# Forgetting attention on one Trainium2 core: score and value items issued in pairs

## The chip, the cores and the metric

The kernel runs on one core of one Trainium2 chip. The metric is the device time of one execution in microseconds, from launch to end, of that core. The kernel before takes 2528.2 us in the median of three runs (2527.69 to 2528.59).

## What is computed

One layer of a streaming encoder over 2048 tokens of width 1024, in 32-bit floats: RMS norm and a combined projection; forgetting attention in 8 heads of width 64 beside a pooling branch; cross attention to 256 memory tokens; a gated feed-forward block. The change touches the forgetting attention alone:

```python
c = jnp.cumsum(jax.nn.log_sigmoid(f_logit), axis=-1)
for start in range(0, S, Q_BLOCK):
    end = start + Q_BLOCK
    s = jnp.einsum('bhqd,bhkd->bhqk', q[:, :, start:end], k[:, :, :end]) * scale
    s = s + c[:, :, start:end, None] - c[:, :, None, :end]
    s = jnp.where(kpos[None, :] <= qpos[:, None], s, -jnp.inf)
    p = jax.nn.softmax(s, axis=-1)
    outs.append(jnp.einsum('bhqk,bhkd->bhqd', p, v[:, :, :end]))
```

## The kernel before

Matrix products in full precision are made of products of a high and a low part (`hi` is a rounded copy, `lo` the difference). Each engine has its own instruction queue and works it off in order. The stages follow one another: projection, pooling and its share of the output projection, forgetting attention, output projection with cross attention, feed-forward. The changed stage runs from about 523 to 903 us of the span.

**Units and items.** The attention is cut into 32 units (h, b): head h (0 to 7) and block b (0 to 3) of 512 query rows. Two generators give out the work in items:

- A *score item* (`score_items`, line 769) is one tile of 128 queries by up to 512 keys: two products of TensorE (PE, line 791) into the PSUM tile `sps` (three buffers), and one operation of VectorE (DVE, line 793) that adds the forget bias, writes the scores to the SBUF row tile `s{b}g{g}` and keeps the row's minimum. GpSimd (POOL) makes the masked bias `cm` (line 782) for a diagonal tile. When a row of tiles is complete, a small reduction on DVE (line 798) and one or two exponentials on ScalarE (ACT, line 803, at most 1024 columns each) follow by appointment.
- A *value item* (in `value_items`, line 843) is one chunk of 128 keys by 512 queries: up to four 128x128 transposes on PE (the helper `turned`, line 55) into the PSUM tile `tp` (three buffers); the rounded copy `ph` on ACT and the difference `pl` on DVE (the helper `sub_hi`, line 63; five buffers each); and, LAG = 3 items later, two products with the values V into `acc` (`weighted`, line 854). Every eighth chunk (`SHARE`) inside a unit is split by POOL in place of DVE (lines 887 to 889) and has a lag of 5.

A unit has 4(b+1) items of each kind, so there are 320 score items and 320 value items. On the diagonal the last four chunks of a unit have 4, 3, 2 and 1 transposes. At a unit's end `drain` issues the products still waiting, and `finish` adds the two halves of `acc` on ACT and DVE.

**The order.** PE, DVE and ACT keep the order in which the Python code issues (`in_order`). A loop draws a score item while `lead` is under LEAD = 22, else a value item, and calls `tick()` after each; `later(n, fn)` issues `fn` n ticks on (EX = 7 for an exponential, 2 more for the row's second one). After 22 scores the loop gives one score item and one value item in turn. In `value_items`, `wait` holds the chunks whose products are still to come; `step()` is called once for each chunk and issues what has come of age:

```python
wait.append([lag, (j, qa, ph, pl)])
step()
yield True
```

POOL and SyncE (SP, which starts most DMAs) take no part in the fixed order.

Of the kernel before, what the change touches and what calls it, by code (L numbers as in the profile page):

```python
# [40 lines left out]
def block_kernel(ctx: ExitStack, tc: tile.TileContext, x, xT, memT, cols, rows, w_qkvf, w_p, w_pool, w_out,  # L41
# [9 lines left out]
    def f(ap):  # L51
        return ap.bitcast(F32)

    def turned(out, src):
        return pe.transpose(out.bitcast(F32R), src, identr[:])  # L55

    def needs(inst, *others):

        for o in others:
            tc.add_manual_dep(inst.ins, o.ins.name, mybir.DependencyInfo(mybir.DependencyClass.Sync, mybir.DependencyReason.DATA))  # L60

    def sub_hi(lo, src, hi, eng=None):
        (eng or dve).tensor_tensor(out=lo, in0=src, in1=f(hi), op=ALU.subtract)  # L63
# [655 lines left out]
    LEAD, LAG = 22, 3  # L719
# [23 lines left out]
    with ExitStack() as c0:  # L743
# [7 lines left out]
        def later(n, fn):  # L751
            due.append([n, fn])

        def tick():
            for e_ in due:
                e_[0] -= 1
            for e_ in [e_ for e_ in due if e_[0] <= 0]:
                due.remove(e_)
                e_[1]()

        def row_tile(b, g, dt):

            n, w_ = f"s{b}g{g}", min(1024, 512 * (b + 1) - 1024 * g)
            t_ = spool.tile([P, 4 * w_ + 2], dt, tag=n, name=n, bufs=1)
            if dt == F32R:
                dve.memset(f(t_[:, 4 * w_:]), 0.0)
            return t_[:, :4 * w_].rearrange("p (q c) -> p q c", q=4)
# [59 lines left out]
        def finish(unit, acc):  # L827
            h, b = unit["u"]
            fo = tpool.tile([DH, 512], F32, tag="fo", name="fo", bufs=3)
            act.copy(fo[:], acc[DH:, :])  # L830
            dve.tensor_tensor(out=fo[:], in0=acc[:DH, :], in1=fo[:], op=ALU.add)
            later(SCALE, lambda: scale(unit, fo))
# [10 lines left out]
        def value_items(unit):  # L843
            h, b = unit["u"]
            v = unit["head"][4]
            nk = 4 * (b + 1)
            acc = aps.tile([P, 512], F32, tag="acc", name="acc", bufs=2)
            wait = []
            state = dict(n=0)

            def weighted(j, qa, ph, pl):
                for pm in (ph, pl):
                    state["n"] += 1
                    pe.matmul(acc[:, qa * P:], lhsT=v[:, j, :], rhs=pm[:, qa * P:], start=state["n"] == 1,  # L854
                              stop=state["n"] == 2 * nk)

            def step(flush=False):
                for e_ in list(wait):
                    e_[0] -= 1
                    if e_[0] < 0 or flush:  # L860
                        wait.remove(e_)
                        weighted(*e_[1])

            for j in range(nk):
                if j % 8 == 0:
                    exps = unit["exps"][j // 8]
                    assert len(exps) == 4
                    rows = row_tile(b, j // 8, F32R)
                q0 = max(0, j - 4 * b)
                qa = min(q0, 2)  # L870
                tp = tps.tile([P, 512], F32, tag="tp", name="tp", bufs=3)
                for q in range(q0, 4):
                    t_ = turned(tp[:, q * P:(q + 1) * P], rows[:, q, j % 8 * P:(j % 8 + 1) * P])
                    if j % 8 == 0:
                        needs(t_, exps[q])
                ph = tpool.tile([P, 512], F32R, tag="ph", name="ph", bufs=5)
                pl = tpool.tile([P, 512], F32R, tag="pl", name="pl", bufs=5)
                if qa < q0:
                    for t_ in (ph, pl):
                        pool.memset(f(t_[:, qa * P:q0 * P]), 0.0)  # L880
                sl = slice(q0 * P, 512)
                nchunk[0] += 1
                lag = LAG
                if nchunk[0] % SHARE == 0 and 0 < j < nk - 4 and not (h == H - 1 and b >= 2):
                    lag += 2
                    pf = tpool.tile([P, 512], F32, tag="pf", name="pf", bufs=2)
                    act.copy(pf[:], tp[:])
                    pool.tensor_tensor(out=ph[:], in0=pf[:], in1=ones[:, 0:1].to_broadcast([P, 512]), op=ALU.mult)
                    sub_hi(pl[:], pf[:], ph[:], pool)
                else:  # L890
                    act.copy(ph[:, sl], tp[:, sl])  # L891
                    sub_hi(pl[:, sl], tp[:, sl], ph[:, sl])
                wait.append([lag, (j, qa, ph, pl)])
                step()
                yield True

            def drain():
                step(True)
                finish(unit, acc)

            later(2, drain)
# [28 lines left out]
        def all_scores():  # L930
            for un in units:
                h, b = un["u"]
                if b == 1 and h + 1 < H:
                    heads[h + 1] = load_head(h + 1, (hpa, hpb)[(h + 1) % 2])
                elif b == 1:
                    load_w_of()
                if b == 3 and h + 1 < H:

                    heads[h + 1] += (load_values(h + 1),)
                un["head"] = heads[h]  # L940
                yield from score_items(un)
            load_cat(0)
            later(4, lambda: split_cat(0))
            load_w_q()

        def all_values():
            for un in units:
                yield from value_items(un)

        with in_order(EN.DVE, EN.Activation):  # L950
            sg, vg = all_scores(), all_values()
            lead, more = 0, True
            while True:
                if more and lead < LEAD:
                    n = next(sg, None)
                    more = n is not None
                    lead += more
                else:
                    n = next(vg, None)
                    if n is None:  # L960
                        break
                    lead -= 1
                tick()
            while due:
                tick()
            for job in rest:
                job()
# [660 lines left out]
```

## Time and profile before

| | |
|---|---|
| median of three runs | 2528.2 us |
| time of the profiled execution | 2526.84 us |
| its span, first to last instruction | 2525.1 us |
| PE busy | 2503.2 us (99%) |
| DVE busy | 1688.4 us (67%) |
| ACT busy | 1241.1 us (49%) |
| POOL busy | 794.5 us (31%) |
| granted clock of PE | 1.00 |

Busy time counts an instruction from its start to its end. Instructions of one engine overlap: a product that is listed with 0.39 us is followed by the next one's start 0.23 us later. What an instruction costs its engine is therefore read from start to start in the timeline, not from its length. Line numbers are those of the kernel before; from line 894 on the changed kernel's are 4 and later 8 higher.

### The profile page before, as it was taken

How to read it: one execution, taken by the hardware profiler on the slowest of the kernel's cores; microseconds unless marked ns; L12 is line 12 of the kernel's file. 1: busy time of each engine (PE TensorE's matmuls, PEld its weight loads, DVE VectorE, ACT ScalarE, POOL GpSimd, SP SyncE). 2: the span in 40 equal slices, each digit the busy share in tenths (PEclk: the TensorE clock that was granted, in tenths of full speed). 3: DMA queues.
4: the chain of work that ended last, by engine and by line, in shares of the span. 5: the costliest groups of instructions: out<-in, count | busy, mean ns of one | idle time of the engine just before them, and what ended most of it. 6: DMA issues, size and time to landing. Idle time of an engine off the chain costs nothing.

```text
span 2525.1 us, 36798 instructions
## 1 busy us (share of the span) xinstructions
PE 2503.2 (99%) x13055; PEld 2142.1 (85%) x13055; DVE 1688.4 (67%) x3000; ACT 1241.1 (49%) x2355; POOL 794.5 (31%) x1096
## 2 busy tenths in 40 slices
PE   9999999999999999999999999999999999999999
PEld 8999999878888878888888888888888888888887
DVE  7444386579999965455877886756776666665554
ACT  6454451069999945444644433335543333333443
POOL 3344310034555623344244554430011212212000
PEclk9999999999999999999999999999999999999999
DMA  6454375364464242222654544457673323325765
GB/s 248 155 153 131 114 245 169 130 175 130 123 167 131 65 141 67 88 88 98 231 206 155 200 164 179 167 189 267 230 256 109 113 96 125 113 96 185 233 207 204
DMA packets 204504, 400.38 MB, mean 159 GB/s; under 512 B 24480, under 2 KB 100000, under 8 KB 193440
## 3 DMA queue, kind: packets, MB, share of 16 engines
q1 hardware_dynamic: 175104, 301.54, 37.3%
q0 software_dynamic: 29216, 96.49, 9.9%
q8 instruction: 102, 1.67, 0.3%
q14 instruction: 82, 0.67, 0.1%
HBM read 273.05 MB, written 129.11 MB: 159 GB/s over the span
## 4 chain that ended last, share of the span: by engine, by line
PE 71%; issue 9%; DVE 2%; POOL 1%; ACT 1%; DMA 0%; POOLq 0%; ACTq 0%; DVEq 0%
PE bk L70 14%; PE bk L68 14%; PE bk L69 14%; PE acc L854 5%; PE sps L791 4%; PE tp L55 3%; PE mmps L68 3%; PE mmps L70 3%; PE mmps L69 3%; PE oo L70 1%; PE oo L68 1%; PE oo L69 1%; PE zp L69 1%; PE zp L68 1%; PE zp L70 1%
## 5 line engine op out<-in xcount | busy, mean ns | idle before, releaser
L63 DVE TENSOR_TENSOR ww<-draw,ww 128x512 fp32r<-128x512 f32 x308 | 204.4, 701 | 155.3 <-ACT ww L190 155.2
L190 ACT CAST ww<-draw 128x512 fp32r<-128x512 f32 x308 | 179.2, 620 | 217.7 <-PE bk L70 170.9
L63 DVE TENSOR_TENSOR ww<-graw,ww 128x512 fp32r<-128x512 f32 x220 | 177.1, 811 | 109.9 <-ACT ww L190 109.7
L69 PE MATMUL bk<-ww,ww 128*128 128x512 f32 x616 | 239.6, 389 | 0.0
L68 PE MATMUL bk<-ww,ww 128*128 128x512 f32 x616 | 239.6, 389 | 0.0
L70 PE MATMUL bk<-ww,ww 128*128 128x512 f32 x616 | 239.6, 389 | 0.0
L190 ACT CAST ww<-graw 128x512 fp32r<-128x512 f32 x220 | 136.0, 622 | 177.7 <-PE bk L70 162.0
L63 DVE TENSOR_TENSOR pl<-tp,ph 128x512 fp32r<-128x512 f32 (+3 forms) x298 | 177.1, 597 | 16.6 <-ACT ph L891 15.5
L68 PE MATMUL zps<-wh,xhi 128*128 128x386 f32 x512 | 175.7, 343 | 0.6 <-DVE qs L186 0.6
L69 PE MATMUL zps<-wl,xhi 128*128 128x386 f32 x512 | 173.5, 339 | 0.0
L70 PE MATMUL zps<-wh,xl 128*128 128x386 f32 x512 | 173.3, 339 | 0.0
L891 ACT CAST ph<-tp 128x512 fp32r<-128x512 f32 (+3 forms) x298 | 147.8, 516 | 12.2 <-PE tp L55 9.1
L68 PE MATMUL bk<-qs,ww 128*128 128x512 f32 x352 | 137.9, 392 | 0.6 <-ACT s L1440 0.6
L70 PE MATMUL bk<-qs,ww 128*128 128x512 f32 x352 | 137.2, 390 | 0.8 <-DVE ww L63 0.8
L1521 POOL DMA_DIRECT2D out_dram<-o x32 | 17.3, 541 | 382.6 <-DVE o L1518 376.9
L69 PE MATMUL bk<-kh,ww 128*128 128x512 f32 x352 | 136.9, 389 | 0.0
L68 PE MATMUL bk<-kl,ww 128*128 128x512 f32 x352 | 136.9, 389 | 0.0
L69 PE MATMUL bk<-cb,ww 128*128 128x512 f32 x352 | 136.9, 389 | 0.0
L70 PE MATMUL bk<-kl,ww 128*128 128x512 f32 x352 | 136.9, 389 | 0.0
L68 PEld LDWEIGHTS bk<-ww,ww 128*128 128x128 f32 x616 | 115.6, 188 | 24.2
L70 PEld LDWEIGHTS bk<-ww,ww 128*128 128x128 f32 x616 | 115.6, 188 | 24.1
L69 PEld LDWEIGHTS bk<-ww,ww 128*128 128x128 f32 x616 | 115.6, 188 | 23.7
(636 smaller groups left out, 7233.7 us busy)
## 6 DMA issues: line engine op xcount, KB each, us to landing
graw<-in_w_gu_dram SPq DMA_DIRECT2D x44, 1024.0 KB, 5.5
draw<-in_w_down_dram SPq DMA_DIRECT2D x66, 256.0 KB, 4.2
xl<-in_xT_dram SPq DMA_DIRECT2D x64, 256.0 KB, 4.7
qkT<-st SPq DMA_DIRECT2D x64, 256.0 KB, 2.6
wdr<-in_w_down_dram SPq DMA_DIRECT2D x22, 512.0 KB, 4.3
vd<-cb SPq DMA_DIRECT2D x16, 512.0 KB, 3.4
qs<-qkT SPq DMA_DIRECT2D x8, 1024.0 KB, 6.8
kh<-qkT SPq DMA_DIRECT2D x16, 512.0 KB, 7.9
```

The source lines that it names most:

```text
L55: return pe.transpose(out.bitcast(F32R), src, identr[:])
L63: (eng or dve).tensor_tensor(out=lo, in0=src, in1=f(hi), op=ALU.subtract)
L68: pe.matmul(ps, lhsT=sh, rhs=mh, start=first, stop=False, skip_group_check=goes_on)
L69: pe.matmul(ps, lhsT=sh, rhs=ml, start=False, stop=False, skip_group_check=goes_on)
L70: pe.matmul(ps, lhsT=sl, rhs=mh, start=False, stop=last, skip_group_check=goes_on)
L190: act.copy(hi, raw)
L791: pe.matmul(ps[:, :wn], lhsT=qs[:, i * P:(i + 1) * P], rhs=kk[:, 512 * c:512 * c + wn], start=(a == 0), stop=(a == 1))
L854: pe.matmul(acc[:, qa * P:], lhsT=v[:, j, :], rhs=pm[:, qa * P:], start=state["n"] == 1, stop=state["n"] == 2 * nk)
L891: act.copy(ph[:, sl], tp[:, sl])
L1521: pool.dma_start(out[rows_, cs], o)
```

## The change

Two places. In `value_items` the chunks are put into `held`, and only after every second chunk are both handed to `wait`, with one `step()` for each. In the loop, a flag `scoring` with a hysteresis of two takes the place of the plain comparison: scores are drawn until `lead` is 22, then value items until it is 20. So the order is two score items, the transposes and splits of two chunks, and then the products of two chunks that have come of age.

```diff
-            wait = []
+            wait, held = [], []
 ...
-                wait.append([lag, (j, qa, ph, pl)])
-                step()
+                held.append([lag, (j, qa, ph, pl)])
+                if j % 2:
+                    for e_ in held:
+                        wait.append(e_)
+                        step()
+                    held.clear()
                 yield True
 ...
-            lead, more = 0, True
+            lead, more, scoring = 0, True, True
             while True:
-                if more and lead < LEAD:
+                if lead >= LEAD:
+                    scoring = False
+                elif lead <= LEAD - 2:
+                    scoring = True
+                if more and scoring:
```

No instruction is added or dropped, no buffer count and no tile shape changes.

## The prediction

> **What bounds the kernel now.** I read the page first, then the windows of the attention stage, then PE's and DVE's timelines inside it, then the waits.
>
> ```profile
> span 2525.1 us, 36798 instructions
> PE 2503.2 (99%) x13055; PEld 2142.1 (85%) x13055; DVE 1688.4 (67%) x3000; ACT 1241.1 (49%) x2355; POOL 794.5 (31%) x1096
> ```
>
> Over the whole span PE is the bound. The change lives in one stage, so that stage has to be read by itself.
>
> ```profile
> core 0: us, PE busy (x) PEld busy (x) DVE busy (x) ACT busy (x) POOL busy (x), PEclk, DMA share, GB/s
> 522.80:902.90 380.10, 373.83 (x2369) 308.46 (x2368) 361.83 (x1153) 347.57 (x750) 200.68 (x363) 1.00 0.47 132
> ...
> 540.00:880.00 340.00, 336.77 (x2161) 282.18 (x2160) 324.59 (x1042) 313.83 (x681) 190.76 (x338) 1.00 0.45 126
> 880.00:903.00 23.00, 21.10 (x138) 15.94 (x137) 21.33 (x47) 19.88 (x39) 3.64 (x8) 1.00 0.43 123
> ```
>
> The stage takes 380.1 us, 15% of the span. In its steady part, 540 to 880, PE is idle 340 - 336.77 = 3.2 us, but DVE only 340 - 324.59 = 15.4 us and ACT 26.2 us. So PE is the bound by a few per cent, with two engines close behind it: whatever PE is spared, DVE caps the gain at some 15 us here.
>
> ```profile
> 708.36 0.39 PE L791 MATMUL sps<-kh,qs 128*128 128x512 f32 x1
> 708.59 0.39 PE L791 MATMUL sps<-kl,qs 128*128 128x512 f32 x1
> 708.82 0.46 PE L55 MATMUL tp<-identr,s3g 128*128 128x128 f32 x4
> 709.12 0.47 PE L854 MATMUL acc<-ph,v 128*128 128x512 f32 x1
> 709.42 0.40 PE L854 MATMUL acc<-pl,v 128*128 128x512 f32 x1
> 709.66 0.39 PE L791 MATMUL sps<-kh,qs 128*128 128x512 f32 x1
> ```
>
> One round of a score item and a value item, from start to start: score product 0.23, the other 0.23, four transposes 0.30, first value product 0.30, second 0.24; in all 709.66 - 708.36 = 1.30 us. The four products have the same shape, yet the one behind the transposes holds PE for 0.30 and the others for 0.23. The next rows tell whether that is the value product or its place.
>
> ```profile
> 875.05 0.39 PE L854 MATMUL acc<-ph,v 128*128 128x512 f32 x1
> 875.28 0.45 PE L854 MATMUL acc<-pl,v 128*128 128x512 f32 x1
> ...
> 889.32 0.80 PE L55 MATMUL tp<-identr,s3g 128*128 128x128 f32 x8
> 889.96 0.47 PE L854 MATMUL acc<-ph,v 128*128 128x512 f32 x1
> ...
> 901.59 0.22 PE L55 MATMUL tp<-identr,s3g 128*128 128x128 f32 x1
> 901.65 0.44 PE L854 MATMUL acc<-ph,v 128*128 128x512 f32 x1
> ```
>
> The value product at 875.05 stands behind a score product and takes 875.28 - 875.05 = 0.23. So it is the place: leaving a run of transposes costs about 0.07. [...]
>
> **The change part by part.** *Exits from transposes.* In the order of the built programs PE leaves a run of transposes 318 times before and 160 times after: 158 fewer. Each saves the 0.07 of the first product. The runs grow from four to eight. Two fours take 2 x 0.30 = 0.60; the run of eight at 889.32 took 0.64 in the stage's last microseconds, where PE also waits; eight at 0.06 to 0.07 each would take 0.48 to 0.56. So the run itself is worth between -0.04 and +0.12, and I take +0.02, near the row of eight, since its excess may be a wait. Together 0.09 a pair (0.03 to 0.19): 158 x 0.09 = **14 us of PE time** (5 to 30), of which 14 x 340/380 = 12.7 in the steady part.
>
> [...]
>
> *DVE.* It does the same instructions in another order: two score operations, then two differences.
>
> ```profile
> 709.38 0.68 DVE L793 CUSTOM_DVE_ANT_0 s1g<-sps,cb 128x512 f32<-128x512 f32 x1
> 709.98 0.08 DVE L793 DVE_READ_ACCUMULATOR2_ANT mx<- 128x1 f32 x1
> 709.98 0.15 DVE L798 TENSOR_REDUCE mx<-mx 128x1 f32<-128x2 f32 x1
> 710.05 0.68 DVE L63 TENSOR_TENSOR pl<-tp,ph 128x512 fp32r<-128x512 f32 x1
> 710.65 0.68 DVE L793 CUSTOM_DVE_ANT_0 s1g<-sps,cm 128x512 f32<-128x512 f32 x1
> ```
>
> Score 0.60, reduction 0.07, difference 0.60: 1.27 a round with a reduction, 1.20 without. A pair costs DVE 2.4 to 2.5 and PE 2 x 1.30 - 0.09 = 2.51 after the change. Where POOL takes over a difference, a pair costs DVE 1.8 to 1.9. So inside long units PE stays just the slower one; at the diagonals and unit ends, where PE's tiles shrink and DVE adds the two halves of `acc`, DVE is. Hence the gain isn't PE's 12.7 in full: DVE's idle time is 15.4, and part of it is the wait for each first copy.
>
> *ACT and the buffers.* The waits say what couples the engines today:
>
> ```profile
> DVE pl L63 <- ACT ph L891: 13.5, 50, 0.7
> PEld tp L55 <- DVE pl L63: 7.9, 23, 1.1
> ACT s3g L803 <- DVE mx L798: 7.7, 21, 0.5
> ...
> ACT ph L891 <- PE tp L55: 6.7, 19, 0.6
> ...
> PEld sps L791 <- DVE mx L793: 1.8, 8, 0.2
> ```
>
> DVE's idle time is mostly the wait for ACT's copy (13.5 us), which in turn waits for PE's transposes (6.7): that part shrinks when PE is faster. PE's own waits for `tp` and `sps` are 9.7 us, and here the change costs slack. Before, a chunk's buffer is needed again three rounds later, 3 x 1.30 = 3.90 us. After, the second chunk of a pair takes the buffer of the first chunk of the pair before. From one to the other PE does two transposings 0.60, four products 0.30 + 3 x 0.23 = 0.99, four score products 0.92, and one transposing 0.30: 2.81. What must happen meanwhile is the transposing (0.46), the copy and the difference:
>
> ```profile
> L63 DVE TENSOR_TENSOR pl<-tp,ph 128x512 fp32r<-128x512 f32 x202 | 137.4, 683 | 12.0 <-ACT ph L891 11.9
> L891 ACT CAST ph<-tp 128x512 fp32r<-128x512 f32 x202 | 114.4, 588 | 6.8 <-PE tp L55 4.0 <-issue 0.5
> ...
> L803 ACT ACTIVATE s3g<-s3g,mx 128x1024 f32<-128x1024 f32 x40 | 46.1, 1154 | 8.7 <-DVE mx L798 8.1
> ...
> L803 ACT ACTIVATE s2g<-s2g,mx 128x1024 f32<-128x1024 f32 x32 | 37.0, 1157 | 0.8 <-PE sps L791 0.5
> L63 POOL TENSOR_TENSOR pl<-pf,ph 128x512 fp32r<-128x512 f32 x22 | 28.4, 1292 | 0.6
> ```
>
> 0.46 + 0.59 + 0.68 = 1.73, so 1.08 us of slack remain, against 2.17 before. PE waits where ACT or DVE is later than that. I cost this at nothing: in the issued order an exponential stands behind a pair's second copy or between its two copies, and PE's products and scores, 0.99 + 0.92 = 1.9 us a pair, lie over it; and while PE waits for DVE, DVE has its next two score operations (1.2 us) to do, so neither starves. Without that cover it is the third rival.
>
> *The lag.* A chunk's product comes three chunks later for the first of a pair and four for the second; five copies are then alive, and there are five buffers. Where POOL splits a chunk (22 times) six would be, so the last copy waits for that chunk's two products: 0.30 + 0.24 + 0.16 of pipeline after its own transposes in place of 0.16, which is 0.54 later. DVE's other difference (0.60) covers that; uncovered it is 22 x 0.54 = 12 us. POOL's two operations on such a chunk get more time than before, not less. The ticks number as many as before, so exponentials, inverses and loads come up at the same counts; SP's and POOL's queues keep their order. What follows the stage begins earlier by what is saved; PE is busy there, too.
>
> *The sum.* Between nothing and 14 us, capped by DVE, I take half: **-7 us**. Against the profiled execution's own time, 2526.84 us (1.7 outside its span), that is 2519.8; the median of the runs is 1.4 higher, so 2528.2 - 7 = **2521**.
>
> **The rivals.** *PE stays the bound throughout.* For it: PE's idle time of 3.2 us in 340. Against: DVE would have to run at 324.59/(340 - 12.7) = 99%. It gives 2528.2 - 14 = 2514.
>
> *Nothing moves.* DVE and ACT already set the pace in the mean, and what PE is spared returns as waits for `tp` and `sps`. For it: DVE at 95%, ACT at 92%. Against: the rounds at 708 to 710 are back to back on PE, with no gap. It gives 2528.
>
> *Slower: the `tp` slack.* One exponential of 1024 columns takes 1.15, more than the slack of 1.08; with the read of its sum, 0.09 from start to start by my estimate (0.19 long, overlapping the next), it lasts 1.25. If it begins just as a pair's first transposes end, the buffer is at least 1.25 - 1.08 = 0.17 late. Today's waits of the kind last 13.5/50 = 0.27 (DVE behind a copy) and 7.9/23 = 0.34 (PE behind a difference); I price one at 0.27. It decides from the point where such exponentials fall there as a rule and DVE has no work stored. There are 80 of them (40, 32 and 8 in units b = 3, 2, 1); at 0.27 each 21 us are lost against 14 won: 2528.2 + 7 = 2535.
>
> [...]
>
> **How the numbers follow.** A measurement of this kernel tells about 0.2% (5 us) from no change: under 2523.1 is faster, over 2533.3 slower. Forecast (DVE takes over part way, 2517 to 2524): 0.42, of which 0.04 lies within 0.2%. PE bound: 0.13. Nothing moves: 0.18. Slack lost: 0.26. Clock: 0.01. Faster is 0.38 + 0.13 = 0.51, same 0.04 + 0.18 = 0.22, slower 0.27. The range runs from 2513 (the upper half of the second case left out, 0.06) to 2536 (0.12 of the fourth and the last left out): 0.19 outside. The forecast's own range is 2517 to 2524.
>
> **What would show it.** Right: eight transposes in a run of 0.5 to 0.6 us; one product of 0.30 and three of 0.23 behind them; the steady part some 7 us shorter, with DVE's busy share up from 95% to about 97% and its wait for ACT's copy down. Wrong: PE's wait for DVE at L55 up from 8 us to over 20 (the slack was needed), DVE's wait for ACT's copy up (exponentials ahead of copies), or exits that cost the same per transpose, so that PE's rounds don't shorten at all.

## The result and the profile after

The changed kernel takes 2544.72 us (median of 6 runs, 2544.07 to 2547.33) against 2528.06 for the kernel before: 16.7 us more, a ratio of 1.007 (95% interval 1.006 to 1.008). It was forecast at 2521 and came out slower. The page of the changed kernel begins:

```profile
span 2544.8 us, 36846 instructions
PE 2505.5 (98%) x13055; PEld 2144.0 (84%) x13055; DVE 1693.5 (67%) x3000; ACT 1241.1 (49%) x2355; POOL 797.0 (31%) x1096
```

The instruction counts of the engines are the old ones. The first and last of the value products stand in these rows of PE (duration min/median/max, then the first and last start):

```profile
L854 PE MATMUL acc<-ph,v x320: 276/398/473, 537.1 to 919.8; 128*128 128x512 f32 x128, 128*128 128x256 f32 x32
L854 PE MATMUL acc<-pl,v x320: 278/392/398, 537.4 to 919.9; 128*128 128x512 f32 x128, 128*128 128x256 f32 x32
```

In the kernel before:

```profile
L854 PE MATMUL acc<-pl,v x320: 276/392/505, 537.4 to 902.9; 128*128 128x512 f32 x128, 128*128 128x256 f32 x32
```

So nearly the whole loss lies in this stage: 919.9 - 902.9 = 17.0 of the 19.7 us between the spans of the two profiled executions. (The profiled execution of the changed kernel, 2546.55, is 1.8 above its median, that of the kernel before 1.2 below.) The stage's windows, with the columns of the prediction's table (the steady part now ends at 895):

```profile
540.00:895.00 355.00, 337.28 (x2153) 283.65 (x2152) 326.80 (x1042) 312.90 (x681) 191.12 (x337) 1.00 0.43 121
895.00:921.00 26.00, 22.89 (x149) 18.46 (x148) 23.80 (x52) 21.46 (x42) 4.37 (x9) 1.00 0.41 128
```

PE's idle time in the steady part rose from 3.2 to 17.7 us, DVE's from 15.4 to 28.2, ACT's from 26.2 to 42.1. No engine has more work; all wait more. The clock is granted in full. PE's timeline shows a pair in which it waits for nothing:

```profile
700.44 0.80 PE L55 MATMUL tp<-identr,s2g 128*128 128x128 f32 x8
701.08 0.46 PE L854 MATMUL acc<-ph,v 128*128 128x512 f32 x1
701.38 0.39 PE L854 MATMUL acc<-pl,v 128*128 128x512 f32 x1
701.61 0.39 PE L854 MATMUL acc<-ph,v 128*128 128x512 f32 x1
701.84 0.39 PE L854 MATMUL acc<-pl,v 128*128 128x512 f32 x1
702.07 0.39 PE L791 MATMUL sps<-kh,qs 128*128 128x512 f32 x1
...
702.99 0.80 PE L55 MATMUL tp<-identr,s2g 128*128 128x128 f32 x8
```

The order is the one the diff asks for, and one product of 0.30 stands in front of three of 0.23. But the run of eight transposes takes 0.64, and two fours took 0.60: the pair takes 702.99 - 700.44 = 2.55 in place of 2 x 1.30 = 2.60. Inside a run the steps, from start to start, are 59 and 64 ns for the first two transposes and about 85 for every further one (medians over the 96 runs of eight; over 220 fours before the change: 59, 64, 85, 85). Two runs in one lose one cheap start.

What the engines wait for in the steady part (us in total, times, longest):

```profile
ACT ph L891 <- PE tp L55: 29.3, 53, 0.8
PEld sps L791 <- DVE mx L793: 25.2, 30, 1.3
...
DVE fo L831 <- ACT fo L830: 13.5, 23, 0.7
PE sps L791 <- DVE mx L793: 13.1, 23, 0.9
DVE pl L63 <- ACT ph L891: 12.3, 42, 0.9
...
ACT ph L891 <- PE acc L854: 5.9, 15, 0.7
...
PE tp L55 <- DVE pl L63: 3.6, 8, 0.7
```

(PE's 23 waits at the `sps` products each end together with one of the 30 at the weight loads, PEld; such a pair counts as one wait.) The wait for `fo` in the kernel before, in the steady part of its stage:

```profile
DVE fo L831 <- ACT fo L830: 0.9, 2, 0.5
```

Two waits are new: DVE waits 13.5 us, in 23 places, for `fo`, ACT's copy of `acc` at a unit's end; and PE waits for DVE at the score products, 13.1 us where there was next to none. A third is new on ACT alone: it waits 5.9 us for products that are to free one of the five `ph`. DVE's wait for the copies `ph` is about what it was. One place where DVE waits for `fo`, first on ACT and then on DVE:

```profile
663.01 0.57 ACT L891 CAST ph<-tp 128x512 fp32r<-128x512 f32 x1
663.48 0.73 ACT L803 ACTIVATE s0g<-s0g,mx 128x512 f32<-128x512 f32 x1
664.11 0.19 ACT L803 ACTIVATION_READ_ACCUMULATOR s0g<-s0g,mx 128x1 f32 x1
664.33 0.58 ACT L830 COPY fo<-acc 64x512 f32<-64x512 f32 x1
```

```profile
663.62 0.69 DVE L63 TENSOR_TENSOR pl<-tp,ph 128x512 fp32r<-128x512 f32 x1 [0.31 <-ACT ph L891]
664.23 0.14 DVE L798 TENSOR_REDUCE mx<-mx 128x1 f32<-128x2 f32 x1
664.94 0.68 DVE L831 TENSOR_TENSOR fo<-acc,fo 64x512 f32<-64x512 f32 x1 [0.57 <-ACT fo L830]
665.55 0.67 DVE L793 CUSTOM_DVE_ANT_0 s1g<-sps,cb 128x512 f32<-128x512 f32 x1
```

ACT does the copy of the next unit's second chunk (to 663.58), an exponential, and only then `fo` (to 664.91). DVE has one difference to do meanwhile, and the addition stands next; the score operation behind it, for which PE is waiting, starts at 665.55. In the kernel before DVE had a score operation ahead of the addition:

```profile
690.03 0.58 ACT L830 COPY fo<-acc 64x512 f32<-64x512 f32 x1
690.06 0.68 DVE L793 CUSTOM_DVE_ANT_0 s3g<-sps,cb 128x512 f32<-128x512 f32 x1
...
690.66 0.68 DVE L831 TENSOR_TENSOR fo<-acc,fo 64x512 f32<-64x512 f32 x1
```

`drain` is due at the second tick from the next unit's first chunk on. Before, those two ticks were a value item and a score item; now they are two value items, and no score operation lies between.

### The profile page after: what moved, and what is told of

It reads as the page before. It is cut to its first block, busy times and chain, and to the rows that moved or that the text cites. A ratio compares the mean times of both kernels' runs of the same rounds, so it can differ in the third digit from the quotient of the medians.

```text
span 2544.8 us, 36846 instructions
## 1 busy us (share of the span) xinstructions
PE 2505.5 (98%) x13055; PEld 2144.0 (84%) x13055; DVE 1693.5 (67%) x3000; ACT 1241.1 (49%) x2355; POOL 797.0 (31%) x1096
## 4 chain that ended last, share of the span: by engine, by line
PE 65%; issue 10%; DVE 5%; ACT 4%; POOL 1%; DMA 1%; SPq 0%; POOLq 0%; ACTq 0%; DVEq 0%
PE bk L70 13%; PE bk L69 13%; PE bk L68 13%; PE mmps L68 3%; PE sps L791 3%; PE mmps L70 3%; PE acc L854 3%; PE mmps L69 3%; PE tp L55 3%; DVE pl L63 1%; PE oo L68 1%; PE oo L69 1%; PE oo L70 1%; ACT ph L891 1%; PE zp L68 1%
## 5 line engine op out<-in xcount | busy, mean ns | idle before, releaser
L63 DVE TENSOR_TENSOR pl<-tp,ph 128x512 fp32r<-128x512 f32 (+3 forms) x298 | 170.4, 596 | 15.4 <-ACT ph L891 13.9
```

## The experiments

Two theories. **Unit ends:** DVE's addition has lost its cover, and PE pays through the three `sps` buffers. **Slack:** pairs ask more of three buffers (`sps`, `tp`) than single items do. The kernel before was run again beside each group of experiments and took 2527.3 to 2527.5 us in the median; the ratios below are against those runs.

**1. Finish later.**

```diff
                 step(True)
-                finish(unit, acc)
+                later(3, lambda: finish(unit, acc))
```

> The changed kernel, with one thing moved: a unit's last products are issued where they were, but finish (ACT's copy of acc, DVE's addition) three ticks later, behind the next pair's two differences. Unit-end theory (DVE stands at each unit's end behind the last products and ACT's copy, 13.5 us of waits, and DVE has no time to spare): 2544.7 falls by about 13 us to some 2531, and DVE's wait for ACT at the addition is gone. Slack theory (three sps and three tp buffers are too few for pairs): 2543 to 2546, no change.

Measured: 2537.35 us (ratio 1.0037, 1.0024 to 1.0050), 7 less than the changed kernel. DVE's wait for `fo` fell from 13.5 to 6.2 us (7 places of 0.9, all behind units of sixteen chunks, where the short unit b = 0 follows). Both fell by 7, about half of what the unit-end theory expected; this speaks for the unit ends, and what the other 10 us are the run doesn't tell.

**2 and 3. Each half of the change alone.** Scores paired, chunks single:

```diff
-                held.append([lag, (j, qa, ph, pl)])
-                if j % 2:
-                    for e_ in held:
-                        wait.append(e_)
-                        step()
-                    held.clear()
+                wait.append([lag, (j, qa, ph, pl)])
+                step()
```

> Only the loop's half of the change: two score items, then two value items, but each chunk's products right behind its transposes, as before. So PE's runs of transposes stay at four and are left 320 times. Unit-end theory: finish falls between the two score items just as in the changed kernel, so most of the loss stays, 2538 to 2545. Slack theory for sps: the same loss, 2538 to 2545; slack theory for tp or the five copies: near 2528, since transposes are apart again.

Measured: 2543.34 us (ratio 1.0059, 1.0043 to 1.0076), nearly the whole loss, with the same pair of waits: DVE for `fo` 12.2 us, PE for DVE at the score products 13.7. One thing is not as the expectation had it: in this run's trace PE leaves a run of transposes 234 times, not 320, and 62 of the runs are of eight. The two value items of a pair follow each other, and where the first has no products to issue yet, as at a unit's start, their transposes still meet. The other half, the diff's first part on the kernel before:

> Only the other half: score and value items in turn, as before, but the products of two chunks together behind every second one. Unit-end theory: finish keeps its place of before, so near 2528 (2524 to 2531). Slack theory for tp and for the five copies: part of the loss, 2533 to 2540; slack theory for sps: near 2528.

Measured: 2530.70 us (ratio 1.0012, 1.0002 to 1.0021), some 3 us slower, and DVE's wait for `fo` is 1.0. The loss comes with the loop's half, as the unit-end theory has it. The 3 us stay within its range and don't fit the slack theory's 2533 or more; here each chunk's transposes still have a score item between them.

**4. A fourth sps buffer**, taken from `acc`.

```diff
-ps = sps.tile([P, 512], F32, tag="s", name="sps", bufs=3)
+ps = sps.tile([P, 512], F32, tag="s", name="sps", bufs=4)
...
-acc = aps.tile([P, 512], F32, tag="acc", name="acc", bufs=2)
+acc = aps.tile([P, 512], F32, tag="acc", name="acc", bufs=1)
```

> [...] Slack theory for sps: PE's 38 us of waits for DVE at the score products mostly go, and the time falls by 8 us or more, to 2537 or less. Unit-end theory: DVE's wait stays, 2543 to 2548; the single acc may add a little, as the next unit's first products wait for the addition.

Measured: 2551.91 us (ratio 1.0093, 1.0078 to 1.0108), slower yet and above both ranges. PE's wait at `sps` has gone, and another has come for it:

```profile
PEld acc L854 <- DVE fo L831: 28.4, 29, 1.4
PE acc L854 <- DVE fo L831: 24.3, 29, 1.3
DVE fo L831 <- ACT fo L830: 14.2, 22, 0.7
```

PE now waits for the late addition itself. That fits score buffers which only pass DVE's lateness on, but doesn't show it, since the single `acc` makes this wait. It also makes the time no measure, and the run says nothing on `tp`.

**5. Only the addition later.** ACT's copy stays where the change put it.

```diff
-            dve.tensor_tensor(out=fo[:], in0=acc[:DH, :], in1=fo[:], op=ALU.add)
-            later(SCALE, lambda: scale(unit, fo))
+            later(2, lambda: add(unit, acc, fo))
+
+        def add(unit, acc, fo):
+            dve.tensor_tensor(out=fo[:], in0=acc[:DH, :], in1=fo[:], op=ALU.add)
+            later(SCALE, lambda: scale(unit, fo))
```

> The changed kernel with one DVE instruction per unit moved: ACT's copy of acc stays, DVE's addition (32 in all) comes two ticks later, behind the next pair's score operations instead of ahead of them. Unit-end theory: DVE's 13.5 us of waits for that copy go, and the time falls by about as much, to 2528 to 2533, below the 2537 of the kernel in which the whole of finish was moved. Slack theory: 2543 to 2546. Nothing of the calculation changes.

Measured: 2535.34 us (ratio 1.0030, 1.0018 to 1.0041): 9.4 of the 16.7 us are back, 2 short of what was expected. DVE's wait for `fo` is gone from the list, and PE waits elsewhere:

```profile
DVE pl L63 <- ACT ph L894: 17.8, 43, 0.9
...
PEld tp L55 <- DVE pl L63: 10.1, 24, 0.6
PEld tp L55 <- ACT pf L890: 7.8, 15, 0.8
...
PE tp L55 <- DVE pl L63: 6.3, 18, 0.5
...
PE tp L55 <- ACT pf L890: 5.7, 15, 0.6
...
PEld sps L791 <- DVE mx L793: 2.9, 10, 0.4
```

(Lines from 831 on are 3 higher here; `pf` is ACT's copy of a chunk that POOL splits.) The wait at `sps` has fallen from 25.2 to 2.9; that at `tp`, which was 3.6 on PE, is now 6.3 + 5.7. This points to a second cause behind the first.

**6. The early drain in the kernel before.**

```diff
-            later(2, drain)
+            later(1, drain)
```

> The kernel before, without any pairing, but with drain one tick earlier, so that the addition stands on DVE directly behind the difference of the next unit's first chunk, with no score operation between, as the changed kernel has it. Unit-end theory: the wait alone brings most of the loss to the old kernel: DVE waits about 0.5 us at 23 or more of 32 units, and the time rises from 2527.5 to 2536 to 2542. Slack theory: within 3 us of 2527.5.

Measured: 2538.96 us (ratio 1.0044, 1.0029 to 1.0059), within the unit-end theory's range, but not by the wait that it named:

```profile
DVE pl L63 <- ACT ph L891: 20.5, 63, 0.7
ACT fo L830 <- PE acc L854: 16.3, 21, 1.9
...
DVE fo L831 <- ACT fo L830: 1.4, 2, 1.2
```

Here ACT stands, in order, in front of a copy of `acc` whose last products are not there yet, and DVE waits for the next `ph`. PE's last products of a unit stand a place earlier as well, and wait 4.2 us for DVE's `pl`. So the place of the unit's end in the order is worth 11.6 us in the old kernel, too; that it is the addition on DVE which costs it is shown by run 5, not by this one.

**7. Scores paired, chunks single, addition later** (runs 2 and 5 together).

> Scores in pairs, transposes and products of single chunks in turn, and the addition two ticks later. Against the kernel with both pairings and the same late addition it differs in PE's runs alone: fours that are left twice in place of eights left once. If a run of eight saves PE 0.09 us a pair and PE counts, this one is slower by up to 10 us; if the saving is 0.03, as the steps of 59, 64 and then 85 ns inside a run say, or DVE is the bound, both lie within 4 us: 2528 to 2535.

Measured: 2530.35 us (ratio 1.0013, 1.0003 to 1.0023). It is 5 us *faster* than run 5, which differs by the pairing of the chunks alone; neither expectation had that. As in run 2, PE leaves its transposes 234 times here, against 160 in run 5, so by 0.03 to 0.05 us an exit run 5 should have been some 2 to 4 us ahead. PE gains nothing visible from runs of eight, and the pairing of the chunks costs. Against run 2, where the chunks are single too, the late addition is worth 2543.34 - 2530.35 = 13.0 us, more than the 9.4 of run 5.

**8. Four tp and two sps**, on run 5.

```diff
-ps = sps.tile([P, 512], F32, tag="s", name="sps", bufs=3)
+ps = sps.tile([P, 512], F32, tag="s", name="sps", bufs=2)
...
-tp = tps.tile([P, 512], F32, tag="tp", name="tp", bufs=3)
+tp = tps.tile([P, 512], F32, tag="tp", name="tp", bufs=4)
```

> The changed kernel with the late addition (2535.3), and one PSUM bank moved from sps to tp: four and two. Slack theory for tp (what is left of the loss is the pair of transposes waiting for ACT and DVE, 30 us of waits on PE): the rest goes, 2527 to 2531. If the waits at tp are only DVE's lateness seen from PE: 2533 to 2537. If two sps are too few for a pair of scores: over 2538.

Measured: 2541.96 us (ratio 1.0056, 1.0039 to 1.0073). The waits at `tp` are gone; at `sps` the load waits for DVE 106 times, 40.5 us in all (10 times and 2.9 us in run 5). So two `sps` are too few for a pair, and whether four `tp` help the run doesn't tell.

**9 and 10. Without the addition**, on the changed kernel and on the kernel before.

```diff
-            dve.tensor_tensor(out=fo[:], in0=acc[:DH, :], in1=fo[:], op=ALU.add)
```

> The changed kernel without DVE's addition at the units' ends (the output lacks the high half of acc): 32 x 0.60 = 19 us of DVE work and the 14 us of waits ahead of it are gone. If DVE's time and that wait make up the loss, it falls to 2510 to 2520 and lies below the old kernel without the addition by the 4 us (0.03 a pair) that PE then has of the pairing; with the 0.09 of the prediction, by 14 us. Slack theory: it stays above the old kernel without the addition, by 5 us or more.

> The kernel before without the same addition (the output lacks the high half of acc), as the measure for the run beside it. If DVE was the bound before, the time falls by 10 us or more, to 2517 or less; if PE was, by no more than the 3 us by which PE is idle, to 2524 or more.

Measured: 2531.96 us (ratio 1.0019, 1.0010 to 1.0029) for the changed kernel and 2526.18 (0.9994, 0.9985 to 1.0003) for the old one. Taking 19 us of work from DVE gave the old kernel about 1 us: **DVE, 95% busy, was not what bounded the stage.** PE, idle for 2.3 of 340 us in run 10's steady part, was. The changed kernel won 12.8 and still lies 5.8 us above its measure, as the slack theory has it and not the other.

**11. A larger share for POOL**, in the kernel before: `SHARE = 6`.

> The kernel before with every sixth chunk in place of every eighth split by POOL, which takes some 8 differences of 0.60 from DVE. If DVE is the bound in the stage, 2 to 5 us faster than before, 2522 to 2526; if POOL's two operations (1.05 and 1.29) come late for their products, no faster: 2527 to 2532.

Measured: 2531.68 us (ratio 1.0018, 1.0008 to 1.0027), slower. No gain from DVE's relief shows, which agrees with run 10; why it is 4 us slower was not followed up.

**12 to 14. Moving the exponentials.** On run 5 the second exponential of a row three ticks behind the first (`EX, X2 = 7, 3` in place of 7, 2), then both a tick later (`8, 2`), and the first of these on run 7.

> The changed kernel with the late addition (2535.3), and a row's second exponential three ticks behind its first in place of two, so that ACT has a copy between the two and no two exponentials stand ahead of a pair's first copy. If what is left of the loss is ACT's copies standing behind exponentials while only 1.1 us of tp slack remain: PE's waits at tp fall from 15 us in six heads to under 9, and the time to 2529 to 2532. If the three tp buffers are too few whatever ACT does: 2534 to 2537.

> The same base, with all exponentials one tick later (8 in place of 7, the second 2 behind), which puts the first of a row ahead of a pair's first copy or between its copies in the other parity. By the theory of ACT's order the time changes with the place, by 2 us or more to either side of 2535, and PE's waits at tp change with it; if the buffers alone decide, 2534 to 2537.

> Scores in pairs, chunks one by one, late addition (2530.4), and the second exponential three ticks behind the first. By the theory of ACT's order there is less to win, since the single chunks leave more slack: 2527 to 2530, level with the kernel before.

Measured: 2533.98 (ratio 1.0024, 1.0015 to 1.0033), 2536.33 (1.0034, 1.0021 to 1.0047) and 2526.86 (0.9998, 0.9988 to 1.0008). With chunks in pairs the place of the exponentials is worth a microsecond or two, and the intervals overlap with run 5: the first expectation is missed, and PE's wait at `tp` hardly moves from the 6.3 + 5.7 of run 5. Run 12:

```profile
PE tp L55 <- DVE pl L63: 6.9, 16, 0.6
...
PE tp L55 <- ACT pf L890: 4.7, 15, 0.6
```

With single chunks 3.5 us went (the intervals of runs 7 and 14 just overlap), and the kernel is level with the one before. Run 14's only wait of PE at `tp`:

```profile
PE tp L55 <- DVE pl L63: 2.8, 8, 0.5
```

The third run against the first, everything else alike: the pairing of the chunks costs 2533.98 - 2526.86 = 7.1 us, and PE waits 11.6 - 2.8 = 8.8 us more at `tp`. The five `ph` do not show as the reason: ACT's wait for products, 5.9 us in the changed kernel, is absent from run 12. Whether the old kernel would gain from the later second exponential, too, was not run.

**15 and 16. A fourth tp buffer with sps left alone.** Runs 9 and 10 with `tp` at four and `acc` at one.

```diff
-acc = aps.tile([P, 512], F32, tag="acc", name="acc", bufs=2)
+acc = aps.tile([P, 512], F32, tag="acc", name="acc", bufs=1)
...
-tp = tps.tile([P, 512], F32, tag="tp", name="tp", bufs=3)
+tp = tps.tile([P, 512], F32, tag="tp", name="tp", bufs=4)
```

> The changed kernel without DVE's addition (the output lacks the high half of acc; 2532.0 with three tp buffers), with a fourth tp buffer, for which acc gives up one of its two. If the pairs of transposes lose their time for want of a tp buffer: PE's 14 us of waits at tp in six heads mostly go, and the time falls to 2523 to 2528, level with or below the kernel before with the same cuts. If ACT and DVE are late in themselves: 2530 to 2533. A wait of the first products for the single acc would show under acc.

> The measure for the run beside it: the kernel before without the addition (the output lacks the high half of acc; 2526.2 with three tp buffers), with four tp buffers and one acc. PE waits little for tp there, so by every theory 2524 to 2528, unless the single acc costs.

Measured: 2527.75 (ratio 1.0000, 0.9991 to 1.0010) and 2524.99 (0.9991, 0.9982 to 1.0001). PE's waits of the changed kernel without the addition, with three `tp` buffers:

```profile
PE tp L55 <- ACT pf L886: 6.2, 14, 0.6
...
PE tp L55 <- DVE pl L63: 3.7, 16, 0.5
```

and with four:

```profile
PEld acc L853 <- ACT fo L830: 11.2, 14, 1.3
PE acc L853 <- ACT fo L830: 9.2, 14, 1.2
...
PEld sps L791 <- DVE mx L793: 3.4, 10, 0.4
```

With the fourth buffer the wait at `tp` is gone altogether and the time falls by 4.2 us, against 1.2 in the old kernel. What is left above the old kernel, 2.8 us, stands beside a new wait for the single `acc`, 9.2 us on PE. The first time lies in the range that goes with a want of `tp` buffers. So three `tp` buffers were too few for pairs of chunks. What pairs would give with four `tp`, three `sps` and two `acc`, nine tiles where the stage's pools hold eight, was not tried.

No version here beats the kernel before by more than the measurement tells: the best that calculates all of the layer, run 14, is level with it.

## Why the prediction was wrong

*Where PE's time goes* was right: the 0.07 behind a run of transposes is there, is paid half as often, and PE was the bound.

*The run of eight* failed as a size. I bounded the run by -0.04 and +0.12 a pair and took +0.02, since I put the 0.64 of the one row of eight down to a wait. It was no wait: the 96 runs of eight in the changed kernel take 0.64 in the median. So a pair saves 0.07 - 0.04 = 0.03 to 0.05 (2.60 to 2.55 by the rows above), not 0.09, and 158 exits are worth 5 to 8 us, not 14. The steps of the fours of the kernel before, 59, 64, 85 and 85, with every further one at 85, give 59 + 64 + 6 x 85 = 633 ns for a run of eight: an estimate from the trace of the kernel before, which the 0.64 bears out.

*"The ticks number as many as before, so exponentials, inverses and loads come up at the same counts"* is the step that cost most. The counts are the same, but what stands under a count isn't: two ticks were a chunk and a score item, and are now two chunks. DVE's addition lost the score operation that had covered ACT's copy. I had not listed `finish` among the moved steps at all. Measured: 9.4 us (run 5; 13.0 with single chunks, runs 2 and 7), through a wait of PE for `sps`.

*"while PE waits for DVE, DVE has its next two score operations (1.2 us) to do, so neither starves"*: the slack of 1.08 us at `tp`, costed at nothing, costs about 7 us (runs 12 and 14; 5.0 by runs 5 and 7). The third rival named that buffer and came nearest to the time, 2535 against 2545, but its price hung on 80 long exponentials ahead of a pair's first copy; moving the exponentials changed 1 to 2 us (runs 12 and 13), and it was the number of buffers that decided (run 15). So its sum came near by luck. Nor did the signs named for it appear: in the changed kernel the load's wait for DVE at L55 was 5.9 us, not over 20, and DVE's wait for ACT's copy did not rise; the wait that grew was PE's at `sps`, and the one at `tp` rose only when the addition was moved. Of the waits at `tp` in run 5 nearly half are for ACT's `pf`, the copy for POOL, on which I had placed no price there.

*The cap.* That DVE's idle time limits the gain was not what counted: with 19 us less to do on DVE the old kernel gained about 1, and the pairs still came out 5.8 behind it (runs 9 and 10). How much DVE would let PE gain where no buffer is short was not measured.

*The clock*, to which the chances give 0.01, played no part: the windows of the stage show a granted clock of 1.00 before and after.

The sum, in one order of undoing: unit ends 9.4 (run 5), second exponentials 1.4 (run 12), paired chunks 7.1 (run 14). That is 17.9 us, from 2544.72 to 2526.86, for a loss of 16.7; the kernel before was itself 0.8 lower beside run 14. PE's small saving is inside the third number. In another order the parts come out otherwise, as if one wait covered another: the late addition is worth 13.0 with single chunks, and the chunks' half alone costs 3 (run 3). The scores' pairing by itself is level with the old kernel, once the addition and the second exponentials are moved (run 14).

## What to carry to other kernels

When the grouping of an order changes, list for everything that comes up by a count what stood between it and the work it waits for, and what stands there now: the same count can mean another neighbour, and an operation that loses its cover stalls an engine in order. Before joining runs of short matmuls, time a long run in the trace by its single steps, and believe a row that is slower than the estimate until its wait is shown. And count buffers by the distance between two uses: pairs cut the distance here from 3.9 to 2.8 us, and busy shares of engines said nothing about that.

## What the runs showed of the hardware

In a run of 128-column transposes, each with weights of its own, PE takes 59 and 64 ns for the first two and about 85 for each one after, and the product of 512 columns that follows holds PE for 0.30 in place of 0.23. From the second on, the weight loads of such a run start 85 ns apart, too (medians over the changed kernel's runs of eight); whether they set the pace no run tests. The granted clock stayed at 1.00 in the windows with runs of 0.64 us.
